# First conv pairs from scaled x while the shift loads, and twenty modulation tiles on TensorE

## The chip, the cores and the metric

The kernel runs on one core of a Trainium2 chip. The metric is device time in microseconds (us). The engines are TensorE (PE; PEld is its weight loads), VectorE (DVE), ScalarE (ACT), GpSimd (POOL) and SyncE (SP), which issues most DMAs.

## The reference, cut to what matters

Two transformer blocks over 256 tokens of width 1024 in float32. Only the head of the first block bears on the change:

```python
mod = silu(c) @ w_ada + b_ada                     # 1024 x 6144
sh1, sc1, g1, sh2, sc2, g2 = split(mod, 6)
h = layer_norm(x) * (1 + sc1) + sh1
z, xbc, dt_raw, sc_b, sc_c, sc_h, gate_a, gate_b = split(h @ w_in)
xbc = silu(causal_depthwise_conv(xbc, ssd_conv_w) + ssd_conv_b)   # 4 taps, 4096 channels
```

Then follow a selective scan over xbc, a short gated convolution, gates, an output projection, a mixture of 64 experts, and a second block (its own `c_2`, `w_ada_2`). Each block needs six modulation rows of 1024, 12 in all. Since the shift is one value per feature for all tokens, (a + sh1) @ W = a @ W + sh1 @ W, and sh1 @ W is one value per output channel.

## The kernel before, in words

**Weights.** `Stream` (L35) loads weights in tiles of 128 x 2048 (1 MB) into a ring of five buffers, `wraw`, through SP in the order in which they were requested; a request waits until a buffer is free (`pump`, L67; `done`, L85). SP's program order is the order of the requests. A linear weight is taken in two halves; each half is split into a high part (`whi`, ScalarE, L196) and a low part (`wlo`, VectorE, L200), both fp32r, three buffers each. `take` (L107) splits one half ahead.

**A pair.** `lin_fm` (L548) makes a pair of 128-channel blocks for 256 tokens: for each half 8 k-tiles times three matmuls (high x high, high weight x low feature, low weight x high feature), so 48 matmuls of 256 columns. The features are `hh` and `hl`, high and low part of h, features on partitions.

**Modulation.** One row of 1024 is a "piece" of four tiles of 1 MB (two k-tiles each). The first two, shift `sh1` = piece (0,0) and scale `sc1` = piece (0,1), are computed by TensorE in `ada_piece` (L395): per k-tile four matmuls with 32 stationary columns in four column groups, 8 per tile, which the trace shows as 16 instructions. The other ten pieces are 40 tiles. They are requested between the weights at places given by strings (L270: x for the 16 conv pairs, s for 12 gated-conv pairs, o for 4, z for 8, g for 8, u for 8) and worked on by `ada_tick` (L410) after the pair of the same place: the first k-tile of a piece on ScalarE (L430), the other seven on VectorE (L432, multiply by silu(c) and add into `adac`, later `adae`), then one sum over partitions with ones on TensorE (L437) and the bias (L392).

**The start.** SP loads c, shift tiles with x behind the second, scale tiles, then the first conv weights. `norm_rows` normalises x, `turn_rows` (L498) transposes it into four PSUM tiles, `to_feature` (L508) scales and shifts them and makes `hh` and `hl`. Every matmul of the conv pairs needs both sc1 and sh1.

**Order.** The order on SP is that of the program. On the other engines a planner takes, by its own costs and due times, the earliest instruction of the program that it holds ready. Once built, each engine runs in order.

**The stages** up to 454 us: start; 16 conv pairs (`xbc_pair`, L621) with four taps on ScalarE and VectorE (L631, L633) and the dt product (L567); 12 gated-conv pairs interleaved with the scan (`ssd`, L654); 4 pairs `pyb`; 8 pairs z; 8 pairs of gates; 4 times two pairs with `w_ssd_out`; `w_o`, whose rows are multiplied by g1 on VectorE (L242).

Of the kernel before, what the change touches and what calls it, by code (L numbers as in the profile page):

```python
# [18 lines left out]
F32 = mybir.dt.float32  # L19
# [7 lines left out]
T = 256  # L27
# [7 lines left out]
class Stream:  # L35
# [31 lines left out]
    def pump(self):  # L67
        while self.issued < len(self.reqs):
            i = self.issued
            load, _, tag = self.reqs[i]  # L70
            tag = tag or (self.free or [None])[0]
            if tag not in self.free:
                break
            self.free.remove(tag)
            self.tag[i] = tag
            pool, depth = self.rings[tag]
            if tag == "whl":
                t = [pool.tile([128, 1024], F32, tag=h, name=f"{h}_{i}", bufs=depth) for h in ("whi", "wlo")]
            else:
                t = pool.tile([128, 2048], F32, tag=tag, name=f"{tag}{i}", bufs=depth)  # L80
            load(t)
            self.raw[i] = t
            self.issued += 1

    def done(self, i):  # L85
        self.left[i] -= 1
        if self.left[i] == 0:
            self.raw.pop(i)
            self.free.append(self.tag[i])
            self.pump()  # L90
# [31 lines left out]
def build(ctx, tc, I, out, dbg=None, stop=None):  # L122
# [44 lines left out]
    V.memset(onescol[:, 7:8], 1.0)  # L167
    V.tensor_scalar(ones_r, jp, 0.0, 1.0, op0=OP.mult, op1=OP.add)
    flip = glob.tile([128, 128], F32, name="flip")
# [34 lines left out]

    def req_cols(w, c0, k0=0):
# [4 lines left out]
        ws.add(f, [lambda t, h=h: t.rearrange("p (k n) -> p k n", k=8)[:, :, 128 * h:128 * h + 128] for h in range(2)])  # L210

# [35 lines left out]
    def req_ada_tile(b, piece, k0):  # L247
        w = I["w_ada_2" if b else "w_ada"][0]

        def f(t):  # L250
            n = 2 if (b, piece, k0) == (0, 1, 6) else 1
            for m in range(n):
                nc.sync.dma_start(t.rearrange("p (k n) -> p k n", k=2)[:, 2 // n * m:2 // n * (m + 1)],
                                  w[k0 * 128:(k0 + 2) * 128, piece * 1024:(piece + 1) * 1024]
                                  .rearrange("(k p) n -> p k n", p=128)[:, 2 // n * m:2 // n * (m + 1)])
            if (b, piece, k0) == (0, 0, 2):
                nc.sync.dma_start(x, I["x"][0].rearrange("(t p) d -> p t d", p=128))

        ada_q[b, piece, k0] = ws.add(f, None)

    def req_ada(b, piece):
        for k0 in range(0, 8, 2):
# [28 lines left out]
    for i, c0 in enumerate(bcols + xcols):  # L291
        req_cols(w_in, c0)
        req_ada_at("x", i)
    for i in range(4):
# [71 lines left out]

    hp3 = keep.tile([128, 3, 32], F32, name="hp3")
    for k, nm in enumerate(("ssd_dt_bias", "ssd_A_log", "ssd_D")):
        a = I[nm][0]
        A.dma_start(hp3[:, k, :], bass.AP(tensor=a.tensor, offset=a.offset, ap=[[0, 128], [1, 32]]))  # L370
    Dcol = keep.tile([128, 16], F32, name="Dcol")
    for j in range(2):
        V.tensor_copy(Dcol[64 * j:64 * j + 64], hp3[64 * j:64 * j + 64, 2, j::2])
    Abc = keep.tile([128, 32], F32, name="Abc")
    A.activation(Abc, hp3[:, 1, :], AF.Exp)
    V.tensor_scalar(Abc, Abc, -1.0, None, op0=OP.mult)


# [11 lines left out]
    def ada_end(b, pc, p):  # L390
        r = work.tile([128, 256], F32, tag="adar", name=f"adar{b}_{pc}", bufs=2)
        V.tensor_add(r, p[:, :256], bada[pc % 2])  # L392
        return r

    def ada_piece(b, pc):  # L395

        ada_bias(b, pc)
        p = paux(f"ada{b}_{pc}")
        for k0 in range(0, 8, 2):
            i = ada_q[b, pc, k0]  # L400
            w = ws.take_raw(i)
            wv = w.rearrange("p (k n) -> p k n", k=2)
            for k in range(2):
                for j in range(4):
                    PE.matmul(p[32 * j:32 * j + 32, :256], cst[:, 8 * b + k0 + k, :], wv[:, k, 256 * j:256 * j + 256],
                              start=(k0 + k == 0), stop=(k0 + k == 7), tile_position=(0, 32 * j))
            ws.done(i)
        return ada_end(b, pc, p)

    def ada_tick(*at):  # L410

        for _ in range(ada_at.get(at, 0)):
# [94 lines left out]

    def to_feature(ps, sc, sh, hi, lo, name):  # L508

        for kp, p in enumerate(ps):  # L510
            f = work.tile([128, 2, 256], F32, tag=("scm", "cu")[kp % 2], name=f"{name}_tf{kp}", bufs=2)
            for k in range(2):
                kk = 2 * kp + k
                scale_shift(k, f[:, k, :], p[:, 256 * k:256 * k + 256], sc[:, kk:kk + 1], sh[:, kk:kk + 1])
            hilo(f, hi[:, 2 * kp:2 * kp + 2, :], lo[:, 2 * kp:2 * kp + 2, :])
# [7 lines left out]
    hh = keep.tile([128, 8, T], F32R, tag="actH", name="hh")  # L523
    hl = keep.tile([128, 8, T], F32R, tag="actL", name="hl")
    ws._split(0)
    to_feature(xnt, sc1, sh1, hh, hl, "h")


# [30 lines left out]


    dt = keep.tile([128, 2, 32], F32, name="dt")
    dA = keep.tile([128, 2, 32], F32, name="dA")
# [4 lines left out]
    def dt_work():  # L567
        wdt = work.tile([128, 8, 32], F32, name="wdt", tag="X", bufs=2)
        with nc.allow_non_contiguous_dma("dt columns"):
# [3 lines left out]
        hilo(wdt, wdh, wdl)  # L573
        pdt = paux("pdt")
# [42 lines left out]

    BC = keep.tile([128, 16, T], F32, tag="big1", name="BC")
    xs = tail.tile([128, 16, T], F32, tag="big2", name="xs")

    def xbc_pair(dst, f0, d0):  # L621

        p = plin()
        lin_fm(p, hh, hl)

        def evac():
            a = work.tile([128, 2, T], F32, tag="cacc", name=f"cacc{f0}", bufs=2)
            for f in range(2):
                fc = f0 + f
                o = f * T  # L630
                A.activation(a[:, f, :], p[:, o:o + T], AF.Identity, bias=cb[:, fc:fc + 1], scale=cw[:, 96 + fc:97 + fc])  # L631
                for s in (1, 2, 3):
                    V.scalar_tensor_tensor(a[:, f, s:], p[:, o:o + T - s],  # L633
                                           cw[:, (3 - s) * 32 + fc:(3 - s) * 32 + fc + 1],
                                           a[:, f, s:], op0=OP.mult, op1=OP.add)
            A.activation(dst[:, d0:d0 + 2, :], a, AF.Silu)

        defer(evac)

    adac = tail.tile([128, 2, D], F32, tag="ga", name="adac")  # L640
    for i in range(16):
        if i < 8:
# [3 lines left out]
        ada_tick("x", i)  # L646
        if i >= 2:
            step()
# [1345 lines left out]
```

## Time and profile before

| | us |
|---|---|
| Median of 3 runs (lowest, highest) | 1335.69 (1335.33, 1337.22) |
| The profiled execution, own time | 1335.36 |
| Its span, first to last instruction | 1333.5 |
| PE / PEld / DVE / ACT / POOL busy | 1265.9 / 1026.6 / 813.2 / 562.3 / 178.3 |
| Mean granted clock of TensorE | 0.981 |

A matmul's end is modelled in this trace: a row of 0.28 us is a matmul that the next one follows after less. The distance of starts is what one costs, and a busy TensorE need not be at its peak. "<-DVE ..." names what ended an engine's idle time.

### The profile page before, as it was taken

Reading aid. Unit: us, or ns where it says so; the run is one execution under the profiler, and the core shown is the slowest. Engines: PE = TensorE matmul, PEld = TensorE weight load, DVE = VectorE, ACT = ScalarE, POOL = GpSimd, SP = SyncE. Lnnn points to the kernel's source line nnn. Section 1 sums busy time; section 2 is a strip of 40 time slices with the busy share of each in tenths; the row PEclk is TensorE's granted clock in tenths of the full one; section 3 lists DMA queues with packets and bytes.
Section 4 is the critical chain, followed back from the end, with each engine's and each line's share of the span. In section 5 each row is a group of like instructions: output and inputs, shape, how many; then the busy total and the mean of one; then the engine's idle time right before and its main releaser. Section 6 shows DMA issues by size and latency. Waiting matters only on the chain.

```text
span 1333.5 us, 22547 instructions
## 1 busy us (share of the span) xinstructions
PE 1265.9 (95%) x8998; PEld 1026.6 (77%) x8998; DVE 813.2 (61%) x1306; ACT 562.3 (42%) x849; POOL 178.3 (13%) x169
## 2 busy tenths in 40 slices
PE   4999999999999989999999999999979998999997
PEld 2989988789899777657576767476548876999985
DVE  2999998977898852222322222222255677788995
ACT  1666644455654341313131313132245655666643
POOL 1001243421100000211112111112120000000000
PEclk9899999999999969999999999999989999999999
DMA  9977867669789287999999999999995334455450
GB/s 338 323 232 254 263 220 239 226 196 320 250 281 362 78 352 296 406 417 419 419 418 413 400 418 419 378 421 403 418 347 179 126 127 141 144 190 190 161 187 32
DMA packets 148975, 380.18 MB, mean 285 GB/s; under 512 B 7839, under 2 KB 97285, under 8 KB 129028
## 3 DMA queue, kind: packets, MB, share of 16 engines
q1 hardware_dynamic: 145856, 373.20, 75.7%
q0 software_dynamic: 2240, 5.34, 1.2%
q8 instruction: 71, 1.16, 0.4%
q10 hardware_dynamic: 772, 0.19, 0.1%
q14 instruction: 36, 0.29, 0.1%
HBM read 377.59 MB, written 1.10 MB: 284 GB/s over the span
## 4 chain that ended last, share of the span: by engine, by line
PE 61%; DVE 5%; DMA 3%; issue 2%; ACT 1%; POOL 0%; POOLq 0%; DVEq 0%; SPq 0%; ACTq 0%
PE gu L1444 16%; PE dn L1475 8%; PE xgp L1402 5%; PE sc L1497 4%; PE pgt L556 2%; PE pgt L557 2%; PE pgt L558 2%; PE pvl L557 2%; PE pvl L556 2%; PE pvl L558 2%; PE pf L908 1%; PE pf L910 1%; PE pf L906 1%; DVE wlo L200 1%; DMA wraw<-in_w_down_dram 1%
## 5 line engine op out<-in xcount | busy, mean ns | idle before, releaser
L196 ACT ACTIVATE whi<-wraw 128x1024 fp32r<-128x1024 f32 x216 | 228.2, 1059 | 239.6 <-PE pf L910 30.8
L200 DVE TENSOR_TENSOR wlo<-wraw,whi 128x1024 fp32r<-128x1024 f32 x216 | 271.4, 1259 | 64.4 <-ACT whi L196 63.0
L1444 PE MATMUL gu<-mraw,xg 128*32 128x256 f32 (+2 forms) x976 | 135.1, 381 | 0.0
L1485 POOL TENSOR_TENSOR y<-yf,y 128x512 fp32r<-128x512 f32 x60 | 76.9, 1282 | 420.8 <-ACT y L1484 420.7
L1454 DVE SCALAR_TENSOR_TENSOR act<-act,gc,gu 128x256 f32<-128x256 f32 x31 | 14.9, 480 | 192.9 <-ACT act L1453 192.9
L1484 ACT ACTIVATE y<-yf 128x512 fp32r<-128x512 f32 x62 | 39.1, 630 | 160.4 <-DVE yf L1483 160.4
L1444 PEld LDWEIGHTS gu<-mraw,xg 128*32 128x32 f32 (+2 forms) x976 | 86.7, 135 | 22.7 <-issue 5.3
L1444 PE MATMUL gu<-wraw,xg 128*32 128x256 f32 (+2 forms) x704 | 98.7, 381 | 0.0
L1483 DVE TENSOR_TENSOR yf<-dn,g 128x512 f32<-128x512 f32 x62 | 42.9, 692 | 66.2 <-PE dn L1475 66.2
L558 PE MATMUL pl<-hh,wlo 128*128 128x256 f32 x256 | 74.3, 291 | 4.2 <-DVE wlo L200 4.1
L1444 PEld LDWEIGHTS gu<-wraw,xg 128*32 128x32 f32 (+2 forms) x704 | 58.2, 129 | 24.1 <-issue 3.9
L556 PE MATMUL pl<-hh,whi 128*128 128x256 f32 x256 | 73.7, 288 | 0.0
L557 PE MATMUL pl<-hl,whi 128*128 128x256 f32 x256 | 73.5, 288 | 0.0
L432 DVE SCALAR_TENSOR_TENSOR adac<-wraw,csil,adac 128x1024 f32<-128x1024 f32 x49 | 66.4, 1355 | 5.1 <-DMA wraw<-in_w_ada_dram 4.5
L1497 PE MATMUL sc<-y,S 128*128 128x512 f32 x248 | 63.3, 404 | 1.4 <-ACT y L1484 0.8
L1497 PEld LDWEIGHTS sc<-y,S 128*128 128x128 f32 x248 | 45.5, 188 | 17.7 <-issue 4.4
L1453 ACT ACTIVATE act<-gu 128x256 f32<-128x256 f32 x31 | 11.9, 384 | 107.3 <-PE gu L1444 107.3
L1404 ACT ACTIVATE xg<-xgp,mvp 128x512 f32<-128x512 f32 (+1 forms) x64 | 48.8, 765 | 19.4 <-PE xgp L1402 19.2
L1402 PE MATMUL xgp<-D,x2h 128*128 128x512 f32 (+1 forms) x128 | 55.5, 434 | 1.4 <-DVE D L1121 1.4
L1475 PE MATMUL dn<-mraw,aT 128*32 128x512 f32 (+2 forms) x200 | 55.4, 596 | 0.0
L558 PEld LDWEIGHTS pl<-hh,wlo 128*128 128x128 f32 x256 | 49.5, 194 | 6.2 <-DVE wlo L200 5.8
L1402 PE MATMUL xgp<-D,x2l 128*128 128x512 f32 (+1 forms) x128 | 53.8, 421 | 0.1
(575 smaller groups left out, 3522.8 us busy)
## 6 DMA issues: line engine op xcount, KB each, us to landing
wraw<-in_w_in_dram SPq DMA_DIRECT2D x56, 1024.0 KB, 6.2
wraw<-in_w_ada_dram SPq DMA_DIRECT2D x47, 1024.0 KB, 7.6
wraw<-in_w_up_dram SPq DMA_DIRECT2D x44, 1024.0 KB, 5.3
wraw<-in_w_down_dram SPq DMA_DIRECT2D x37, 1024.0 KB, 10.0
mraw<-in_w_up_dram SPq DMA_DIRECT2D x32, 1024.0 KB, 14.5
mraw<-in_w_gate_dram SPq DMA_DIRECT2D x28, 1024.0 KB, 7.1
mraw<-in_w_down_dram SPq DMA_DIRECT2D x23, 1024.0 KB, 17.4
wraw<-in_w_gate_dram SPq DMA_DIRECT2D x21, 1024.0 KB, 15.1
```

What stands on the lines that cost most here:

```text
L196: A.activation(hi, v, AF.Copy)
L200: V.tensor_sub(lo, v, hi.bitcast(F32))
L432: V.scalar_tensor_tensor(acc, wv[:, k, s_], c, acc, op0=OP.mult, op1=OP.add)
L556: PE.matmul(o, wh[:, k, :], xh[:, k0 + k, :], start=(k == 0), stop=False)
L557: PE.matmul(o, wh[:, k, :], xl[:, k0 + k, :], start=False, stop=False)
L558: PE.matmul(o, wl[:, k, :], xh[:, k0 + k, :], start=False, stop=(k == 7))
L1402: PE.matmul(p[:, :c1 - c0], src[:, t, j::8], Dt[:, t, c0:c1], start=(q == 0), stop=(q == 3))
L1404: A.activation(xg[:, j, c0:c1], p[:, :c1 - c0], AF.Identity, scale=mvp[:, 1, j:j + 1], bias=mvp[:, 0, j:j + 1])
L1444: PE.matmul(p[c * k:c * k + c, off:off + 256], xg[:, j, 128 * bb + c * k:128 * bb + c * k + c], wt[j], start=(j == 0), stop=(j == 7), tile ...
L1475: last_dn[0] = PE.matmul(pd[h][c * k:c * k + c, :], aT[:, j, c * k:c * k + c], wt[j][:, 512 * h:512 * h + 512], start=(j == 0), stop=(j == ...
L1485: last_sub[0] = (V if b >= LAST else G).tensor_sub(y[:, 1, hs_], yf[:, h, :], y[:, 0, hs_].bitcast(F32))
L1497: PE.matmul(p, St[:, bb + m, 128 * t:128 * t + 128], y[:, k, 512 * h:512 * h + 512], start=(q == 0), stop=(q == 2 * len(ys) - 1))
```

## The change

- The scale tiles are loaded first, with x behind the first of them; then the weights of the first three conv pairs (NF = 3), into rooms of their own (not ring buffers); then the shift tiles; then the stream as before.
- x times scale, without shift, is split into `vv[0]` (high, ScalarE) and `vv[1]` (low, VectorE), and also kept in float32 (`scaled`). The first three pairs take `vv` for their features. TensorE's order for this part is written out: the first pair with k outside and its two halves inside, shift tiles in `ada_rows` between the halves of pairs 2 and 3.
- When the shift is there, TensorE multiplies it with the raw weights of the three pairs (`prow`); `shift_cols` turns the rows into columns, `shift_evac` corrects the first three tokens and adds the rest as a bias in Silu. `hh` and `hl` are made from `scaled` and the shift for all later work.
- The first five of the ten pieces (20 tiles, those of stages x, s and o) go to TensorE in `ada_tick`, in `ada_rows`. The strings change; each stage keeps its number of tiles.
- The three small DMAs of dt bias, A and D, with what hangs on them, come after the features; the dt weights load after the norm. Constants are put ahead of the norm's statistics. `cst` goes: the stationary columns are a broadcast of `csil`.

```diff
@@ Stream.pump
+            if isinstance(tag, tuple):
+                load(tag[0])
+                self.raw[i] = tag[0]
+                self.tag[i] = None
+                self.issued += 1
+                continue
@@ requests
-            n = 2 if (b, piece, k0) == (0, 1, 6) else 1
+            n = 2 if (b, piece, k0) == (0, 0, 6) else 1
-            if (b, piece, k0) == (0, 0, 2):
+            if (b, piece, k0) == (0, 1, 0):
                 nc.sync.dma_start(x, ...)
-    req_ada(0, 0)
-    req_ada(0, 1)
+    req_ada(0, 1)
+    NF = 3
+    w01 = tail.tile([128, 2, 2048], F32, tag="big2", name="w01")
+    wrooms = [w01[:, 0, :], w01[:, 1, :], tail.tile([128, 2048], F32, tag="yb", name="w2")]
+    for i in range(NF):
+        req_cols(w_in, XBC0 + 2048 + 256 * i, 0, (wrooms[i],))
+    req_ada(0, 0)
-   "0110110110110110,010101010101,1111,11111111,11111111,10101010"
+   "0000111101111011,110111100000,1111,11111111,11111111,01010101"
@@ modulation
+    def ada_rows(p, b, pc, k0):
+        i = ada_q[b, pc, k0]
+        wv = ws.take_raw(i).rearrange("p (k n) -> p k n", k=2)
+        for k in range(2):
+            c = csil[:, 8 * b + k0 + k:8 * b + k0 + k + 1].to_broadcast([128, 32])
+            for j in range(4):
+                PE.matmul(p[32 * j:32 * j + 32, :256], c, wv[:, k, 256 * j:256 * j + 256],
+                          start=(k0 + k == 0), stop=(k0 + k == 7), tile_position=(0, 32 * j))
+        ws.done(i)
@@ ada_tick
+            if n < ADA_PE:                      # ADA_PE = 5
+                if k0 == 0:
+                    ada_acc[0] = pacc(f"ada{b}_{pc}")
+                ada_rows(ada_acc[0], b, pc, k0)
+                if k0 == 6:
+                    ada_row(ada_end(b, pc, ada_acc[0]), b, pc)
+                continue
@@ start
     norm_rows(x, xn, 1e-5, "ln0")
-    r0 = ada_piece(0, 0)
-    sh1 = ada_cols(r0, "sh1")
     xnt = turn_rows(xn, "h")
-    r1 = ada_piece(0, 1)
-    sc1 = ada_cols(r1, "sc1", 1.0)
-    ws._split(0)
-    to_feature(xnt, sc1, sh1, hh, hl, "h")
+    sc1 = ada_cols(ada_piece(0, 1), "sc1", 1.0)
+    for kp, p in enumerate(xnt):
+        for k in range(2):
+            kk = 2 * kp + k
+            A.activation(vv[:, 0, kk, :], p[...], AF.Copy, scale=sc1[:, kk:kk + 1])
+            V.scalar_tensor_tensor(vv[:, 1, kk, :], p[...], sc1[:, kk:kk + 1], vv[:, 0, kk, :], op0=OP.mult, op1=OP.subtract)
+        if kp == 1:
+            ws._split(0)
+        for k in range(2):
+            if k:
+                V.tensor_scalar(scaled[kp][:, k, :], p[...], sc1[:, kk:kk + 1], None, op0=OP.mult)
+            else:
+                A.activation(scaled[kp][:, k, :], p[...], AF.Copy, scale=sc1[:, kk:kk + 1])
@@ after lin_fm: three() is its three matmuls on vv, taps() the four conv taps
+    ada_bias(0, 0)
+    pe_order = tc.manual_schedule(engines={mybir.EngineType.SP, mybir.EngineType.PE})
+    pe_order.__enter__()
+    pf = [plin(f"pl{i}") for i in range(NF)]
+    p0b = paux("pl0b")
+    wv_ = [ws.take(), ws.take()]
+    for k in range(8):
+        for f in range(2):
+            three((pf[0] if f == 0 else p0b)[:, :T], wv_[f], k)
+    psh1 = paux("ada0_0")
+    ada_rows(psh1, 0, 0, 0)
+    for i in (1, 2):
+        for f in range(2):
+            w = ws.take()
+            for k in range(8):
+                three(pf[i][:, T * f:T * f + T], w, k)
+                if (i, f, k) == (2, 1, 3):
+                    sh1 = ada_cols(r0, "sh1")
+            if (i, f) != (2, 1):
+                ada_rows(psh1, 0, 0, 2 + 2 * (2 * (i - 1) + f))
+            if (i, f) == (2, 0):
+                r0 = ada_end(0, 0, psh1)
+            if f == 0:
+                for g in range(2):
+                    taps(...)                   # of the pair before
+    for i in range(NF):                         # shift times raw weights, into prow0, prow1
+        for k in range(8):
+            j = k % 4
+            PE.matmul(o[32 * j:32 * j + 32, :], sh1[:, k:k + 1].to_broadcast([128, 32]), w[:, k, :],
+                      start=(k < 4), stop=(k >= 4), tile_position=(0, 32 * j))
+    pe_order.__exit__(None, None, None)
+    ws._split(0)
+    for kk in range(8):
+        f = scaled[kk // 2][:, kk % 2, :]
+        turned = (A.activation(hh[:, kk, :], f, AF.Identity, bias=sh1[:, kk:kk + 1]),
+                  V.scalar_tensor_tensor(hl[:, kk, :], f, sh1[:, kk:kk + 1], hh[:, kk, :], op0=OP.add, op1=OP.subtract))
@@ conv loop
-    for i in range(16):
+    for i in range(NF, 16):
+        if i == NF + 1:
+            shift_cols()
+        elif i in (NF + 2, NF + 3, NF + 4):
+            shift_evac(i - NF - 2)
...
-        if i >= 2:
+        if i >= NF + 1:
             step()
```

`shift_cols` copies `prow` out of PSUM, makes six one-column products with a column `selc` that has a one at every 32nd partition, and forms per-channel constants. `step` advances the dt chain and the scan.

## Rows read from the trace of the kernel before

**Rows 1.** The page's chain that ended last, shares of the span by engine.
```profile
PE 61%; DVE 5%; DMA 3%; issue 2%; ACT 1%; POOL 0%; POOLq 0%; DVEq 0%; SPq 0%; ACTq 0%
```
**Rows 2.** Busy time by stretch: length, PE, PEld, DVE, ACT, POOL, clock, DMA, GB/s.
```profile
15.00:35.50 20.50, 13.82 (x150) 6.63 (x151) 8.19 (x20) 2.98 (x6) 1.91 (x3) 0.95 1.05 392
35.50:57.40 21.90, 21.90 (x167) 21.59 (x166) 19.02 (x26) 13.36 (x18) 0.00 (x0) 0.89 0.94 327
57.40:144.00 86.60, 82.39 (x662) 79.43 (x660) 82.72 (x146) 57.61 (x80) 10.96 (x8) 0.98 0.79 258
144.00:239.00 95.00, 90.00 (x758) 84.64 (x757) 90.31 (x108) 46.94 (x68) 33.92 (x22) 1.00 0.71 231
239.00:282.80 43.80, 39.23 (x322) 34.23 (x321) 39.03 (x41) 17.93 (x29) 17.26 (x15) 1.00 0.66 218
282.80:392.50 109.70, 108.24 (x862) 98.97 (x860) 92.91 (x120) 61.56 (x79) 13.16 (x17) 1.00 0.82 270
```
**Rows 3.** Waits of TensorE, 57.4 to 282.8 us: total us, times, longest.
```profile
PE yp L717 <- DVE Cs L706: 6.2, 4, 2.1
PE pl L558 <- DVE wlo L200: 4.1, 5, 2.9
PE yp L713 <- DVE E L691: 1.4, 1, 1.4
...
```
**Rows 4.** Timeline of the start, 30.5 to 37.5 us: start, length, instruction.
```profile
30.60 0.64 PE L405 MATMUL ada<-wraw,cst 128*32 128x256 f32 x8 [0.98 <-DMA wraw<-in_w_ada_dram]
...
31.87 0.41 PE L452 MATMUL ac_sc<-ident,adar 128*128 128x128 f32 x2 [0.64 <-DVE adar L392]
...
32.52 1.48 ACT L496 ACTIVATE h_tf<-h_tp,sh,sc 128x256 f32<-128x256 f32 x3 [17.89 <-DVE sc L455]
...
34.41 1.06 ACT L196 ACTIVATE whi<-wraw 128x1024 fp32r<-128x1024 f32 x1
...
34.57 0.42 PE L576 MATMUL pdt<-hh,wdh 128*32 128x256 f32 x1 [2.29 <-ACT hh L488]
...
35.49 1.23 DVE L200 TENSOR_TENSOR wlo<-wraw,whi 128x1024 fp32r<-128x1024 f32 x1 [0.25 <-ACT whi L196]
...
35.73 0.41 PE L556 MATMUL pl<-hh,whi 128*128 128x256 f32 x1
```
**Rows 5.** Busy time by stretch, around the first conv matmuls.
```profile
33.40:40.30 6.90, 5.42 (x25) 4.92 (x26) 6.65 (x11) 6.90 (x11) 0.00 (x0) 0.51 1.08 371
```
**Rows 6.** Timeline of TensorE around one closing sum.
```profile
76.92 0.28 PE L556 MATMUL pl<-hh,whi 128*128 128x256 f32 x1
77.13 0.64 PE L437 MATMUL ada<-adac,ones_r 128*32 128x256 f32 x8
77.70 0.38 PE L557 MATMUL pl<-hl,whi 128*128 128x256 f32 x1
77.92 0.28 PE L558 MATMUL pl<-hh,wlo 128*128 128x256 f32 x1
```
**Rows 7.** Timeline of TensorE in one pair after another, first and last row.
```profile
392.97 0.28 PE L556 MATMUL pya<-ynh,whi 128*128 128x256 f32 x1
...
403.52 0.28 PE L557 MATMUL pya<-ynl,whi 128*128 128x256 f32 x1
```
**Rows 8.** Timeline of TensorE: two modulation tiles in a row.
```profile
24.30 1.93 PE L405 MATMUL ada<-wraw,cst 128*32 128x256 f32 x32
```
**Rows 9.** Groups by line, 35.5 to 282.8 us: busy us, mean ns, idle before.
```profile
L432 DVE SCALAR_TENSOR_TENSOR adac<-wraw,csil,adac 128x1024 f32<-128x1024 f32 x40 | 54.8, 1370 | 2.1 <-DMA wraw<-in_w_ada_dram 1.9
...
L196 ACT ACTIVATE whi<-wraw 128x1024 fp32r<-128x1024 f32 x66 | 69.8, 1059 | 78.8 <-PE pl L557 26.2 <-PE pyb L557 22.7 <-PE ph L557 15.6
...
L430 ACT ACTIVATE adac<-wraw,csil 128x1024 f32<-128x1024 f32 x6 | 6.9, 1142 | 3.6 <-DMA wraw<-in_w_ada_dram 3.6
```
**Rows 10.** Timeline of VectorE, 421 to 431 us: the last modulation tile's first half.
```profile
422.11 1.41 DVE L432 SCALAR_TENSOR_TENSOR adae<-wraw,csil,adae 128x512 f32<-128x512 f32 x2 [0.70 <-DMA wraw<-in_w_ada_dram]
```

More of the change, by code (lines that the diff above doesn't have):

```diff
@@ L86, in done @@
         self.left[i] -= 1
-        if self.left[i] == 0:
+        if self.left[i] == 0 and self.tag[i]:
             self.raw.pop(i)
@@ L365, in bcast_row @@
         return t
[L367 to L376, printed above, removed]
     bada = [keep.tile([128, 256], F32, name=f"bada{k}") for k in range(2)]
@@ L399, in ada_piece @@
         for k0 in range(0, 8, 2):
[L400 to L407, printed above, removed]
+            ada_rows(p, b, pc, k0)
         return ada_end(b, pc, p)
@@ L558, in lin_fm @@
                 PE.matmul(o, wl[:, k, :], xh[:, k0 + k, :], start=False, stop=(k == 7))
+    BC = keep.tile([128, 16, T], F32, tag="big1", name="BC")
+    ca = tail.tile([128, NF, 2, T], F32, tag="ga", name="ca")
+    cw4 = cw.rearrange("p (t f) -> p f t", t=4)[:, 16:16 + 2 * NF, :]
+    cws = keep.tile([128, 2 * NF, 4], F32, name="cws")
+    V.tensor_copy(cws[:, :, 0], cw4[:, :, 0])
+    for k in (1, 2, 3):
+        V.tensor_add(cws[:, :, k], cws[:, :, k - 1], cw4[:, :, k])
+    selc = keep.tile([128, 1], F32, name="selc")
@@ new lines, in three @@
+    def three(o, w, k):
+        wh, wl = w
+        PE.matmul(o, wh[:, k, :], vv[:, 0, k, :], start=(k == 0), stop=False)
+        PE.matmul(o, wh[:, k, :], vv[:, 1, k, :], start=False, stop=False)
+        PE.matmul(o, wl[:, k, :], vv[:, 0, k, :], start=False, stop=(k == 7))
+    ada_bias(0, 0)
[4 more added lines that the diff above has]
+    wv_ = [ws.take(), ws.take()]
@@ new lines, in build @@
+    prow1 = [paux("prow0"), paux("prow1")]
+    for i in range(NF):
+        o = prow1[i // 2][:, 256 * (i % 2):256 * (i % 2) + 256]
+        w = wrooms[i].rearrange("p (k n) -> p k n", k=8)
+        for k in range(8):
[3 more added lines that the diff above has]
+    pe_order.__exit__(None, None, None)
+    hh = keep.tile([128, 8, T], F32R, tag="actH", name="hh")
@@ new lines, in build @@
+    hl = keep.tile([128, 8, T], F32R, tag="actL", name="hl")
+    ws._split(0)
+    for kk in range(8):
+        f = scaled[kk // 2][:, kk % 2, :]
+        turned = (A.activation(hh[:, kk, :], f, AF.Identity, bias=sh1[:, kk:kk + 1]),
+                  V.scalar_tensor_tensor(hl[:, kk, :], f, sh1[:, kk:kk + 1], hh[:, kk, :].bitcast(F32),
+                                         op0=OP.add, op1=OP.subtract))
+    hp3 = keep.tile([128, 3, 32], F32, name="hp3")
+    for k, nm in enumerate(("ssd_dt_bias", "ssd_A_log", "ssd_D")):
+        a = I[nm][0]
+        with tc.issue_after(turned[0].ins):
+            A.dma_start(hp3[:, k, :], bass.AP(tensor=a.tensor, offset=a.offset, ap=[[0, 128], [1, 32]]))
@@ new lines, in build @@
+    Dcol = keep.tile([128, 16], F32, name="Dcol")
+    for j in range(2):
+        with tc.issue_after(turned[1].ins):
+            V.tensor_copy(Dcol[64 * j:64 * j + 64], hp3[64 * j:64 * j + 64, 2, j::2])
+    Abc = keep.tile([128, 32], F32, name="Abc")
+    A.activation(Abc, hp3[:, 1, :], AF.Exp)
+    V.tensor_scalar(Abc, Abc, -1.0, None, op0=OP.mult)
+    with tc.issue_after(turned[0].ins), tc.issue_after(turned[1].ins):
+        for g in range(2):
+            taps(ca[:, 2], pf[2], 20 + g, g)
@@ new lines, in build, with shift_cols @@
+    rws = [work.tile([128, 512], F32, tag="E", name=f"rws{i}", bufs=3) for i in range(2)]
+    pcb = paux("pcb")
+    cbias = keep.tile([128, 2, 2 * NF], F32, name="cbias")
+    cedge = keep.tile([128, 2 * NF, 3], F32, name="cedge")
+    def shift_cols():
+        for i in range(2):
+            n = 256 * (NF - 2 * i) if i else 512
+            V.tensor_copy(rws[i][:, :n], prow1[i][:, :n])
+            for m in range(n // 128):
+                PE.matmul(pcb[:, 4 * i + m:4 * i + m + 1], rws[i][:, 128 * m:128 * m + 128], selc, start=True, stop=True)
+        V.tensor_copy(cbias[:, 0, :], pcb[:, :2 * NF])
+        V.tensor_mul(cbias[:, 1, :], cbias[:, 0, :], cws[:, :, 3])
+        for t in range(3):
+            V.tensor_mul(cedge[:, :, t], cbias[:, 0, :], cws[:, :, 2 - t])
@@ L628, in evac @@
             for f in range(2):
[L629 to L635, printed above, removed]
+                taps(a, p, f0 + f, f)
             A.activation(dst[:, d0:d0 + 2, :], a, AF.Silu)
```

59 lines of the change are left out of this document (37 added, 22 removed).

## The prediction

> **What bounds the kernel now.** I read the chain's shares first [rows 1]: TensorE is on the chain far more than anything else. Then busy time by stretch [rows 2], because the change lies in the first 454 us only and shares of the whole span hide it. Four things stand there. Up to 35.5 us the DMA rows are full (share 1.05, 392 GB/s), and TensorE works in pieces. From 35.5 us on TensorE is busy nearly always. From 57.4 to 282.8 us it is idle for 4.2 + 5.0 + 4.6 = 13.8 us (length minus busy time of three rows). In the same three rows VectorE is busy 82.7 of 86.6, 90.3 of 95.0 and 39.0 of 43.8 us. So two engines are nearly full there, and the question is which one sets the pace. The waits of TensorE [rows 3] name VectorE, but their sum is 11.7 us of 225. In the other direction ScalarE waits 78.8 us in front of its weight splits, most of it for matmuls to give the split buffers back [rows 9]: the splits run ahead of TensorE. TensorE therefore sets the pace between the waits of rows 3, and work added to it has to be paid for; work taken from VectorE is worth at most the waits.
>
> **The start.** Today the last modulation tile is used at 30.60 us and ScalarE begins on the features at 32.52 [rows 4]. After the change four tiles fewer are loaded ahead of that point: 4.19 MB at 392 GB/s [rows 2] is 10.7 us, so the last scale tile is used at 19.9. It is whole and no longer halved, 0.4 us more (8 instructions more, worked out below), and 1.9 us follow as today: the features begin at 22.2.
>
> What has to happen before the conv matmuls flow: ScalarE's Copies, in program order, are vv 0 and 1, one scaled, vv 2 and 3, the first weight split, then one scaled, two vv, one scaled, two vv, one scaled, and only then the split of the second half. Twelve at 0.49 us (1.48 for three) and two splits at 1.06 [rows 4] are 8.0 us, and the VectorE half of the second split adds 1.2, less overlap: some 8.8 us after the features begin, that is 31.0 us. The order on TensorE is written out, and in it the second half stands right behind the first three matmuls (k outside, f inside), so the first half, ready at about 26, can't run ahead. Today the flow begins at 35.73 [rows 4]. The gain is 4.7 us, not the 10.7 of the loads. Bounds: 9 us if the planner puts the second split ahead of the later Copies, 3 if the scale comes a little later.
>
> Against it stands work on TensorE that today lies in its idle time ahead of 35 us, or isn't there. A row of 32 instructions of the modulation kind takes 1.93 us [rows 8], one of 8 takes 0.64 [rows 6]: 24 instructions are 1.29 us, so 8 stream in 0.43. In the middle of conv matmuls 8 of them push the next but one matmul from 0.24 to 1.00 us (76.92 to 77.92, rows 6): 0.76. A tile has 16, so 0.76 + 0.43 = 1.19 us. The four shift tiles are 4.8 us. The raw-weight rows are three times 16 of the same kind, with one pair of edges: 3 x 0.86 + 0.3 = 2.9. The two transposes for the shift's columns are 0.4; the six one-column products later some 1.0 (an estimate, between 0.5 and 2).
>
> Steady pace of the conv matmuls: 88 steps from 392.97 to 403.52 are 0.12 us each [rows 7]. Today 167 recorded instructions, three pairs (144) and the dt product, are done at 57.4 [rows 2]. After: 31.0, and 138 matmuls left x 0.12 = 16.6, the low clock again 2.0 (granted 0.51 up to 40.3, rows 5, so the first 4.5 us of the flow ran at 1.2 GHz), 4.8, 2.9 and 0.4 give 57.7, and the dt product, which now needs the shift, is still to come: 24 x 0.12 = 2.9, and the 1.0. That is 61.6 against 57.4: **+4.2 us**, bounds -3 and +7. The features with shift cost eight ScalarE and eight VectorE operations more (4 us each side by side), behind the last conv half and the raw rows; I take them as hidden, and 2 us are late if not.
>
> One rule bears on the clock. The 0.51 was granted after TensorE had stood idle from 32.3 to 34.6 [rows 4, 5]. The Trainium skill, "TensorE: Matmul & The Clock Gate", section "Part 1: The HAM clock gate", says that low is the default and that activity lifts it; the trace agrees (idle, then 0.51). By it the first pair pays the 2.0 us again, as counted; if the scale tiles kept the clock up it would be 2.0 less.
>
> **Twenty tiles on TensorE.** Removed from VectorE: today a piece of four tiles takes one ScalarE operation (1.14 us) and seven on VectorE (1.37), [rows 9]; five pieces are 35 x 1.37 = 48 us of VectorE and 5.7 of ScalarE. Removed from TensorE: five closing sums of 0.76, 3.8 us. Added to TensorE: 20 tiles of 0.86 (streaming alone) to 1.19 (both edges). Some stand beside the scan's matmuls, which have such edges already; I take 1.1: 22.0 - 3.8 = **+18.2 us**, bounds +13.5 and +22.
>
> The row shows 0.76 us for 8 instructions where 0.43 streams, so 0.33 at the two edges. The Trainium skill, "TensorEngine Tiling (Array Packing)", section "Key Properties", says that a change of tiling mode drains the engine; the trace agrees, with those 0.33 us. By the rule at every tile the term is 20.0, without it 13.5.
>
> What the freed VectorE gives back: the 13.8 us of idle time, and 1.7 us of low clock (0.98 over 86.6 us, rows 2) that follows the longest wait: 15.5. The stretch from 282.8 to 392.5, with less on VectorE, still has 1.5 us of idle time, so not all goes; I take **-14 us**. Bounds: -6 (the waits for Cs and E come from a chain ScalarE-VectorE-TensorE, not from load alone), -20 (ends of matmuls are modelled, so some waits may not show). What is late next: with VectorE at 70-75% nothing but TensorE. New waits: a tile on TensorE that hasn't landed stops the conv matmuls queued behind it, where today VectorE waited (2.1 us in all, rows 9); a piece's first tile waits for the sum of the piece before to leave its only bank, a pair of matmuls earlier. Nothing for both, up to 4 in the range.
>
> **The other edits.** Four modulation requests move behind the second of two weight loads near 400-425 us. VectorE's four accumulations of the last tile, 0.7 us each [rows 10], then fall where it is busy without a gap, as gating and splitting of the next weights start: 0 to 2.9 us, I take **+0.6**. Three small DMAs of ScalarE's queue and the 128 KB dt load leave the start and come later: VectorE's first constants no longer wait for one of them, and nothing on the path needs them; 0, gain bounded by 1.5 us on the scale tiles. The stretches from 282.8 on keep their work, and their start moves with the end of this one.
>
> **Sum.** 4.2 + 18.2 - 14.0 + 0.6 = +9.0 us. The profiled execution took 1335.36 us (span 1333.5 and 1.9 around it), 0.3 below the median of the runs. 1344.4; I say 1344.5.
>
> **Rivals.** *VectorE is what sets the pace.* For it: its three rows are as full as TensorE's, and every wait in rows 3 but small ones names it. Then the second split comes early (start -1), the tiles cost what they stream (+13.5), and all waits, hidden ones too, go (-19): -6.5, about 1329. Against it: the 78.8 us that ScalarE waits for TensorE. It decides if TensorE's added work stays under some 22 us beside 20 regained; chance 0.24. *It cancels.* Start +2, tiles at 1.0 (+16.2), waits -18: +0.2, about 1335.7; chance 0.16. *The waits stay.* If the scan's waits are latency and tiles are late on TensorE, -6 takes the place of -14 and 4 us come on top: +21 at worst, with tiles at 1.0 and a start of +3 about +15, 1350; chance 0.13. *The change doesn't do what it says*, in that the planner holds the first pair until the shift is there: the flow would begin no earlier than today, +4.7 more, 1349; in the range of the one before. My forecast, +3 to +13 us, has the remaining 0.47.
>
> **Range and chances.** This kernel's runs can tell about 0.2% (2.7 us) from no change. Slower by more: 0.47 + 0.13 = 0.60; within: 0.16; faster: 0.24. The range reaches the first rival at its upper end and the third nearly whole: 1329 to 1354; the forecast's own is 1338 to 1349.
>
> **What would show it.** Start right: first conv matmul of the flow near 31 us with a gap of several us behind the first three, fourth pair near 58; wrong if the flow begins below 28. Tiles right: some 1.1 us between the conv matmuls on either side of a tile; wrong if below 0.9. Waits right: VectorE near 75% busy from 60 to 280 us, idle time of TensorE below 3 us there, and the z stage beginning some 8 us later than today. If it begins earlier, the sum is wrong on its sign.

## The result, and the profile after

The changed kernel took 1347.03 us (median of 13 runs, 1341.12 to 1354.52) beside 1339.36 us of the kernel before on the same chip (13 runs, 1334.15 to 1343.39): ratio 1.0064, 95% interval 1.0042 to 1.0085. It is slower by 0.64%, or 8.6 us (the medians alone differ by 7.7); the forecast was +9.0 us on 1335.36. The profiled execution took 1350.54 us (span 1348.7), 15.2 more than the one before: 7.7, and it lies 3.5 above its own median while the one before lies 4.0 below its own. A difference between two single profiles is therefore not yet a cost, and what follows takes each part from several kernels.

The chain of waits of the kernel after, shares of the span by engine, against [rows 1]:
```profile
PE 85%; DVE 6%; DMA 4%; issue 2%; ACT 1%; POOL 1%; SPq 0%; DVEq 0%; POOLq 0%; ACTq 0%
```
The two rows can't be held against each other. The chain of the kernel before can be followed back only to 356.49 us (974 of 1333.5 us, its shares add up to 72%), that of the kernel after to 0.74 us; from 420 us on TensorE has 85% of either. So [rows 1] says nothing of the stretch that the change touches, and what sets the pace there has to be read from busy time and waits. Busy time by stretch of the kernel after, columns as in [rows 2]:
```profile
15.00:35.50 20.50, 13.79 (x89) 11.43 (x88) 9.50 (x18) 7.43 (x15) 0.64 (x2) 0.75 1.06 376
35.50:57.40 21.90, 21.90 (x233) 17.63 (x232) 15.00 (x27) 11.78 (x20) 0.55 (x1) 1.00 0.83 262
57.40:144.00 86.60, 86.60 (x792) 79.88 (x791) 71.67 (x148) 57.03 (x82) 7.15 (x6) 1.00 0.79 260
144.00:239.00 95.00, 93.96 (x834) 84.54 (x834) 67.07 (x85) 42.87 (x63) 26.85 (x23) 1.00 0.66 211
239.00:282.80 43.80, 41.63 (x360) 35.07 (x359) 31.82 (x37) 18.50 (x30) 19.03 (x16) 1.00 0.59 200
```
From 57.4 to 282.8 us TensorE's idle time fell from 13.8 to 3.2 us (0 + 1.0 + 2.2), the clock of the first of these stretches rose from 0.98 to 1.00, and VectorE is busy 170.6 of 225.4 us, 76%. What TensorE still waits for there (total us, times, longest), where [rows 3] had 11.7 us, and the two groups by line that answer to [rows 9]:
```profile
PE yp L838 <- DVE Cs L827: 1.6, 2, 1.0
PE pyb L571 <- DVE vv L502: 1.2, 1, 1.2
PE yp L834 <- DVE E L812: 0.3, 1, 0.3
```
```profile
L200 ACT ACTIVATE whi<-wraw 128x1024 fp32r<-128x1024 f32 x59 | 62.4, 1057 | 77.2 <-PE pl L571 18.3 <-PE ph L571 17.4 <-PE pc L571 12.2
...
L445 DVE SCALAR_TENSOR_TENSOR adac<-wraw,csil,adac 128x1024 f32<-128x1024 f32 x1 | 1.7, 1671 | 0.9 <-ACT adac L443 0.9
```
Nearly all of the 40 wide accumulations are gone from VectorE, and ScalarE still waits 77.2 us in front of its weight splits, as it did 78.8 us before. TensorE, not VectorE, paces this stretch.

The start of the kernel after, timeline of TensorE, and then of ScalarE, against [rows 4]:
```profile
26.32 0.55 PE L596 MATMUL pl<-vv,whi 128*128 128x256 f32 x1 [4.55 <-DVE h_tf L538]
...
27.36 0.41 PE L597 MATMUL pl0b<-vv,whi 128*128 128x256 f32 x1
29.39 0.58 PE L598 MATMUL pl0b<-vv,wlo 128*128 128x256 f32 x1 [1.61 <-DVE wlo L204]
29.77 0.42 PE L596 MATMUL pl<-vv,whi 128*128 128x256 f32 x1
...
30.41 0.41 PE L596 MATMUL pl0b<-vv,whi 128*128 128x256 f32 x1
...
53.89 2.80 PE L632 MATMUL prow<-w,sh 128*32 128x256 f32 x48
56.62 0.39 PE L570 MATMUL pl<-hh,whi 128*128 128x256 f32 x1
...
62.30 0.28 PE L572 MATMUL pl<-hh,wlo 128*128 128x256 f32 x1
62.42 1.39 PE L670 MATMUL pcb<-selc,rws 128*128 128x1 f32 x12
63.67 0.36 PE L570 MATMUL pl<-hh,whi 128*128 128x256 f32 x1
```
```profile
22.01 1.57 ACT L530 ACTIVATE vv<-h_tp,sc 128x256 fp32r<-128x256 f32 x4 [17.73 <-DVE sc L468]
23.45 1.07 ACT L200 ACTIVATE whi<-w 128x1024 fp32r<-128x1024 f32 x1
24.40 0.49 ACT L540 ACTIVATE h_tf<-h_tp,sc 128x256 f32<-128x256 f32 x1
24.76 1.23 ACT L530 ACTIVATE vv<-h_tp,sc 128x256 fp32r<-128x256 f32 x3
25.83 1.10 ACT L200 ACTIVATE whi<-w 128x1024 fp32r<-128x1024 f32 x1
```
The features begin at 22.01 (counted: 22.2). The second weight split (the second L200) comes at 25.83, ahead of the last Copies, where the prediction had put it behind all of them; TensorE stops for its lower half for 1.61 us after five matmuls and flows from 29.39. The clock of the flow's first part, same columns as the stretches:
```profile
25.40:35.60 10.20, 7.66 (x34) 7.40 (x35) 5.86 (x11) 4.04 (x8) 0.00 (x0) 0.50 1.04 404
```
One modulation tile between the conv matmuls, timeline of TensorE, against [rows 6]:
```profile
78.83 0.28 PE L572 MATMUL pl<-hh,wlo 128*128 128x256 f32 x1
79.04 1.07 PE L403 MATMUL ada<-wraw,csil 128*32 128x256 f32 x16
80.04 0.39 PE L570 MATMUL pl<-hh,whi 128*128 128x256 f32 x1
80.27 0.28 PE L571 MATMUL pl<-hl,whi 128*128 128x256 f32 x1
```
From 78.83 to the next but one matmul it is 1.44 us where 0.24 is the steady pace: a tile costs 1.2 us, the upper of the two bounds.

### The profile page after: what moved, and what is told of

Read it like the earlier page. It is cut to its first block, busy times and chain, and to the rows that moved or that the text cites. A ratio compares the mean times of both kernels' runs of the same rounds, so it can differ in the third digit from the quotient of the medians.

```text
span 1348.7 us, 23251 instructions
## 1 busy us (share of the span) xinstructions
PE 1291.1 (96%) x9338; PEld 1038.5 (77%) x9338; DVE 781.2 (58%) x1298; ACT 562.4 (42%) x859; POOL 169.8 (13%) x169
## 4 chain that ended last, share of the span: by engine, by line
PE 85%; DVE 6%; DMA 4%; issue 2%; ACT 1%; POOL 1%; SPq 0%; DVEq 0%; POOLq 0%; ACTq 0%
PE gu L1565 16%; PE dn L1596 8%; PE xgp L1523 5%; PE sc L1618 4%; PE pl L570 2%; PE ada L403 2%; PE pl L571 2%; PE pl L572 2%; PE pgt L570 2%; PE pgt L571 2%; PE pgt L572 2%; PE pvl L570 2%; PE pvl L572 2%; PE pvl L571 2%; PE pf L1029 1%
## 5 line engine op out<-in xcount | busy, mean ns | idle before, releaser
L200 ACT ACTIVATE whi<-wraw 128x1024 fp32r<-128x1024 f32 x210 | 221.9, 1058 | 251.4 <-PE pf L1031 30.8
L204 DVE TENSOR_TENSOR wlo<-wraw,whi 128x1024 fp32r<-128x1024 f32 x210 | 259.2, 1235 | 99.9 <-ACT whi L200 93.3
L570 PE MATMUL pl<-hh,whi 128*128 128x256 f32 x208 | 59.4, 285 | 0.0
L571 PE MATMUL pl<-hl,whi 128*128 128x256 f32 x208 | 58.3, 280 | 0.0
L572 PE MATMUL pl<-hh,wlo 128*128 128x256 f32 x208 | 58.2, 280 | 0.0
L1596 PE MATMUL dn<-wraw,aT 128*32 128x512 f32 (+2 forms) x208 | 51.9, 596 | 1.3 <-DMA wraw<-in_w_down_dram 1.3
L570 PE MATMUL pgt<-h3h,whi 128*128 128x256 f32 x176 | 50.7, 288 | 0.6 <-ACT h3h L502 0.6
```

Of the source, the lines that this page charges most:

```text
L200: A.activation(hi, v, AF.Copy)
L204: V.tensor_sub(lo, v, hi.bitcast(F32))
L570: PE.matmul(o, wh[:, k, :], xh[:, k0 + k, :], start=(k == 0), stop=False)
L571: PE.matmul(o, wh[:, k, :], xl[:, k0 + k, :], start=False, stop=False)
L572: PE.matmul(o, wl[:, k, :], xh[:, k0 + k, :], start=False, stop=(k == 7))
L1596: last_dn[0] = PE.matmul(pd[h][c * k:c * k + c, :], aT[:, j, c * k:c * k + c], wt[j][:, 512 * h:512 * h + 512], start=(j == 0), stop=(j == ...
```

## Experiments

All of these compute the whole reference. "Measured" gives the ratio to the kernel before on the same chip, with its 95% interval; times at a place come from the one profile of each kernel. Three marks are used: the start of the flow of conv matmuls, of the fourth conv pair, and of the z stage. With the new start the dt product (24 x 0.12 = 2.9) and the one-column products (62.30 to 63.67 less one step, 1.25), 4.1 us, lie behind the fourth pair; with the old they lie ahead of it or don't exist.

**The twenty tiles alone.**
```diff
 # kernel before
+ADA_PE = 5
+if n < ADA_PE: ada_rows(ada_acc[0], b, pc, k0) ...   # five pieces of four tiles on TensorE
```


> The kernel before with nothing changed but the twenty tiles of stages x, s and o on TensorE (strings and start as before). Theory (TensorE sets the pace there): 20 tiles cost some 1.2 us each and five closing sums of 0.76 go, +20; TensorE's idle time from 57 to 283 us falls from 13.8 to about 2 us; the z stage begins 4 to 8 us later than the 282.9 us of before, and the whole is 0.3 to 0.6% slower. Rival (VectorE sets the pace): the z stage begins 3 to 7 us earlier and the whole is faster by 0.2 to 0.5%.


Measured: 1.0057 [1.0039, 1.0075]. The z stage began at 288.0 where it was 282.9. TensorE's idle time over 57.4 to 282.8 us is 3.15 and VectorE's busy time 169.7, as in the kernel after; busy time over the one stretch:
```profile
57.40:282.80 225.40, 222.25 (x1966) 201.03 (x1965) 169.68 (x253) 114.72 (x166) 54.09 (x44) 1.00 0.68 226
```
Tiles alone bring most of the loss. "VectorE sets the pace" would have made this kernel faster; it falls.

**The start with four tiles.**
```diff
 # kernel after
-ADA_PE = 5
+ADA_PE = 1
```


> The changed kernel with only the first piece (4 tiles) on TensorE, the other 16 tiles back on VectorE. Theory: the fourth conv pair begins where it does in the changed kernel (56.6 us) and the start alone costs 3 to 4 us; the z stage begins near 287 to 291 us, since what TensorE saves (16 x 1.2 less 3.0, 16 us) comes back as waits for VectorE of 10 to 16 us; whole 0.2 to 0.6% slower than before. Rival (VectorE sets the pace): VectorE has 16 x 2.6 = 41 us more, and the z stage begins 10 us or more later than the 290 of the changed kernel; over 1% slower than before.


Measured: 1.0041 [1.0024, 1.0059]; z stage at 286.5, 3.8 us ahead of the kernel after. With sixteen tiles back on VectorE its busy time and TensorE's idle time return (12.5 us):
```profile
57.40:282.80 225.40, 212.90 (x1784) 198.58 (x1783) 204.54 (x298) 124.58 (x178) 58.23 (x43) 0.98 0.72 238
```

**The first pair's halves one after the other.**
```diff
 # kernel after, first pair
-for k in range(8):
-    for f in range(2):
+for f in range(2):
+    for k in range(8):
```


> The changed kernel, first conv pair with its first half's 24 matmuls ahead of the second half's. Theory: the flow begins near 26.3 us and not 29.4, since only the second half waits for its split; the fourth pair begins 2 to 3 us earlier than 56.6, near 54, and the whole is 2 to 3 us below the changed kernel. Rival (the scaled features arrive too late for a half on its own, or the low clock lasts as long as before): fourth pair at 56 or later, no gain.


Measured: 1.0035 [1.0017, 1.0053]. The flow begins at 25.9 instead of 29.4. The fourth pair begins at 53.3; over all profiles it is 52.9 to 54.0 us in three with this order and 54.7 to 56.6 in four with the other, so the loop order costs about 2 us.

**The u requests.** In the kernel after moved back, and in the kernel before moved alone:
```diff
 # us_back: kernel after          # u_only: kernel before, the other way round
-"...,11111111,01010101"
+"...,11111111,10101010"
```


> The changed kernel with the modulation requests of the last eight places (u) as before, behind the first of two weight loads. Theory: the way from the first w_ssd_out matmul to the last of w_o is 0 to 3 us shorter than in the changed kernel; nothing before it moves. Rival: that stretch is the same or longer, and the 2 us that the changed kernel takes more there come from elsewhere.

> The kernel before with nothing changed but the places of the modulation requests among the w_ssd_out loads, as in the changed kernel. Theory: from the first w_ssd_out matmul to the last of w_o it takes 73.5 us and not 71.5 (four profiles with the new places show 73.2 to 73.6 but for none, six with the old ones 71.0 to 71.9), nothing ahead of it moves, whole +0.1 to +0.2%. Rival: that stretch is longer only where stages x to o were changed too; here 71.5.


Measured: 1.0053 [1.0033, 1.0072] for the first, beside 1.0064 with the requests moved; 1.0017 [0.9997, 1.0038] for the second. Neither ratio by itself tells it from nothing. The stretch from the first matmul of w_ssd_out to the last of w_o does: 73.6 (kernel after), 73.2 (halves one after the other), 73.6 (four tiles) and 73.4 us (requests alone) with the new places, 71.0 to 72.0 in the nine profiles with the old. One more kernel with the new places, further below, has 71.8. The cause in the kernel after, timeline of VectorE and of TensorE:
```profile
420.11 0.68 DVE L502 TENSOR_TENSOR ml<-mg,mh 128x512 fp32r<-128x512 f32 x1
427.12 0.75 DVE L445 SCALAR_TENSOR_TENSOR adae<-wraw,csil,adae 128x512 f32<-128x512 f32 x1 [6.32 <-DMA wraw<-in_w_ada_dram]
427.79 1.22 DVE L204 TENSOR_TENSOR wlo<-wraw,whi 128x1024 fp32r<-128x1024 f32 x1
```
```profile
429.06 0.39 PE L572 MATMUL pya<-ynh,wlo 128*128 128x256 f32 x1 [2.39 <-DVE wlo L204]
```
VectorE stands 6.32 us in front of a modulation tile that hasn't landed. Queued behind it is the split of a weight (427.79), and TensorE waits 2.39 us for that split, where the kernel before lost 0.5 us at this place. The requests alone show the same two rows (6.26 and 2.16 us). What makes up the rest of the 2 us differs: in the requests alone and in the four tiles a low clock follows that wait, in the other two TensorE waits once more, at the start of w_o. Busy time of the requests alone, and timeline of TensorE in the kernel after:
```profile
426.10:429.50 3.40, 3.40 (x19) 3.40 (x18) 3.37 (x6) 0.41 (x1) 0.00 (x0) 0.50 0.62 187
```
```profile
456.01 0.51 PE L1027 MATMUL pmix<-whi,mh 128*128 128x512 f32 x1 [0.78 <-DVE adar L393]
```

**Eight tiles, in two places, and twelve.** Pieces are numbered 0 to 4 in the order of use: 0 and 1 lie in the conv stage, 2 between 120 and 157 us, 3 and 4 behind that, in the scan's stage.
```diff
 # kernel before with the code of twenty tiles
-if n < ADA_PE:
+if n in (0, 1):        # tiles8_x;  (3, 4): tiles8_so;  (2, 3, 4): tiles12_so
```


> The kernel before with the first two pieces (8 tiles, all in the x stage) on TensorE. Theory (a tile costs TensorE 1.2 us and gives back only the waits that stand in its own stage): 8 x 1.2 less two closing sums is 8.0 us; the x stage has 4.1 us of waits and 1.7 of low clock to give back; the gated-conv pairs begin 2 us later than the 143.8 of before and the z stage 2 to 3 us later than 282.9; whole +0.1 to +0.3%. Rival (the first tiles taken from VectorE are worth most, whatever their stage): z stage 2 to 5 us earlier.

> The kernel before with the fourth and fifth piece (the last 4 tiles of the s stage and the 4 of the o stage) on TensorE. Theory: again 8.0 us, against 4.9 us of waits in the s stage and 4.4 in the o stage, of which 2 to 3 stay (the scan's own chain): z stage between 1 us earlier and 3 us later than 282.9. If the hidden waits are as large as the visible ones: 3 to 5 us earlier, and this is faster than before. Rival (what a tile gives back is the same anywhere): the same as with the 8 tiles in the x stage.

> The kernel before with the third to fifth piece on TensorE (2 tiles at the end of x, 6 of s, 4 of o). Theory: 12 x 1.2 less three sums is 12.1 us against at most 9.3 of visible waits: z stage 3 to 6 us later than 282.9, whole +0.2 to +0.4%. Rival (VectorE sets the pace in s and o): z stage earlier than with 8 tiles.


Measured: 0.9979 [0.9964, 0.9994], 0.9978 [0.9960, 0.9997] and 1.0051 [1.0030, 1.0072]. Eight tiles in either place are faster than the kernel before by about 0.2%; that was not expected. Twelve, with piece 2 among them, lose nearly as much as twenty. Busy time by stretch with eight tiles in the conv stage, to be held against [rows 2]:
```profile
57.40:144.00 86.60, 86.60 (x768) 81.48 (x767) 74.49 (x139) 55.34 (x77) 7.16 (x6) 1.00 0.84 273
144.00:239.00 95.00, 90.30 (x761) 85.05 (x760) 87.61 (x104) 49.11 (x69) 33.70 (x24) 1.00 0.68 222
239.00:282.80 43.80, 39.23 (x323) 34.31 (x322) 39.03 (x41) 17.91 (x28) 16.89 (x14) 1.00 0.66 215
```
All 4.2 us of idle time of the conv stage went, and with it the 3.4 us at 0.50; the scan's remained. What such a stretch costs can be read from the start of the kernel after: at 0.50 the conv matmuls follow each other after 0.213 us (29.77 to 30.41, three steps), where 0.12 is the steady pace, so 44% of it is lost, 1.5 us of 3.4. The table has the time up to the z stage with this taken off, from the first matmul of the flow (old start) or from the fourth pair less the 4.1 us (new start). For the kernel before: 282.85 - 35.73 = 247.1, with 8.0 us at 0.50 (35.7 to 40.3, and 3.4 from 101.7 on), less 3.5, is 243.6.

| tiles on TensorE | old start, from the flow | new start, from the fourth pair |
|---|---|---|
| 0 | 243.6 (before), 243.6 (requests alone) | |
| 4 | | 224.0 |
| 8 | 244.9 (conv), 244.4 (scan), 244.1 (conv, later normalization) | 223.1 |
| 12 | 249.4 (pieces 2, 3, 4) | 227.6 (pieces 0, 3, 4) |
| 20 | 250.2 | 229.5 (kernel after) |

Eight tiles add 8 x 1.2 - 2 x 0.76 = 8.1 us to TensorE and make this part about 1 us longer; the idle time that the rows show gave back 4.5 of these in the first of them, and where the rest came from isn't shown. Nor is it shown how a part that is 1 us longer belongs to a kernel that is 0.2%, some 2.8 us, faster. The low clock that goes with the waits is not in the table: it cost 1.5 us in the kernel before, 4.5 in the requests alone, whose code up to there is the same, and 0, 1.5 and 3.0 in the three kernels with eight tiles. How often it comes over many executions isn't known. Piece 2 finds no wait to fill: with pieces 3 and 4 TensorE is idle 4.2 us up to 144 and 1.3 us from there to 239, and with piece 2 as well 4.4 and 1.3, so its tiles are paid in full: 4 x 1.2 - 0.76 = 4.0 us of the 5.0 between 244.4 and 249.4. The ratio rises by more, 0.0073 or 9.8 us; 3.0 us of that profile are a low clock in the gates stage (below), and the rest isn't shown. Sixteen tiles, eight in each place, were not tried.

**The new start in its best form.**
```diff
 # kernel after, halves one after the other, u requests moved back
-if n < ADA_PE:
+if n in (0, 3, 4):     # start_so;  start8: ADA_PE = 2
```


> The changed kernel with the first pair's halves one after the other, the u requests as before, and TensorE tiles only for pieces 1, 4 and 5 (12 tiles; 8 of the twenty are back on VectorE). Theory: fourth pair near 53.3 us as with the halves apart; eight tiles fewer on TensorE save it 8.0 us and bring back up to 5.8 of waits in the x stage: z stage near 284 to 286 us (286.9 with the halves apart and twenty tiles), whole between 0.1 and 0.4% slower than before. Rival (VectorE sets the pace in x): z stage at 288 or later.

> The changed kernel with the first pair's halves apart, the u requests as before, and only the first two pieces (8 tiles) on TensorE. Theory: against twelve tiles (-0.07%, z stage at 287.2) four tiles fewer save TensorE 4 us and give back some of the scan's waits: z stage at 284 to 287, whole -0.2 to +0.1%. Rival: the start is worth nothing, and it is as the 8 tiles without it, -0.2%.


Measured: 0.9993 [0.9978, 1.0008] and 1.0005 [0.9986, 1.0023]. The first was expected slower by 0.1 to 0.4% with the z stage at 284 to 286; it isn't slower, though the z stage began at 287.2. With eight tiles the fourth pair begins at 52.9, where four profiles of the old start without tiles ahead of it have 57.4 to 58.9: of 4.5 to 6.0 us, 4.1 go to the products behind the mark. The z stage begins at 281.7, against 283.2 with eight tiles in the conv stage and the old start (285.1 in another execution of the same code up to there, 3.0 of it low clock). The time isn't better than without the new start (0.9979), and where its 1.5 us go isn't settled: from the last matmul of w_o to the end, which no edit touches, single profiles lie between 866.1 and 875.1 us.

**The normalization of the gates stage one pair later.** In the kernel after, the gates stage (first gate matmul to first of w_ssd_out) took 57.9 us where it was 53.7, with TensorE waiting, and then this, by stretch:
```profile
345.30:403.10 57.80, 55.47 (x419) 51.40 (x418) 49.52 (x72) 32.06 (x41) 3.87 (x6) 0.94 0.79 257
...
366.70:373.50 6.80, 6.80 (x30) 6.36 (x31) 3.99 (x7) 3.04 (x5) 0.00 (x0) 0.50 0.52 157
```
The waits of TensorE in that stage of the kernel after, and below them those of the kernel with the edit:
```profile
PE prs L929 <- ACT rsh L502: 1.4, 1, 1.4
PE pg L572 <- DVE wlo L204: 0.9, 1, 0.9
```
```profile
PE prs L929 <- ACT rsh L502: 0.7, 1, 0.7
PE pg L572 <- DVE wlo L204: 0.4, 1, 0.4
PE prs L930 <- DVE rsl L502: 0.2, 1, 0.2
```
The theory was that the wait for the group scale pulls the clock down. The edit calls the normalization's matmuls a pair later:
```diff
 # gates stage: kernel after (norm_late); kernel before with pieces 0, 1 (tiles8_norm_late)
-else:
-    gnorm(i - 1)
+elif i >= 2:
+    gnorm(i - 2)
 ...
+gnorm(6)
 gnorm(7)
```


> The changed kernel with the normalisation of the scan's groups one pair of gate matmuls later. Theory: TensorE's wait of 2.3 us for the group scale goes, the granted clock stays at its upper level through the gates, and the stretch from the first gate matmul to the first w_ssd_out matmul is 53 to 55 us and not 57.8; whole 2 to 4 us below the changed kernel, 0.3 to 0.5% above before. Rival (the low clock there has another cause): a low stretch near 366 us stays, 57 us.

> The kernel before with the first two pieces on TensorE (8 tiles, x stage) and the normalisation one pair later. Theory: the wait of 1.0 to 1.6 us in the gates goes and low clock there can't follow: 1 to 3 us below the kernel before, beyond the 8 tiles' own -0.2%: -0.2 to -0.4%. Rival: the later normalisation makes the first w_ssd_out matmuls wait for the last groups, 1 to 3 us; then the same as before.


Measured: 1.0029 [1.0011, 1.0047] beside 1.0064 [1.0042, 1.0085] without it (another series); and 0.9981 [0.9960, 1.0003] beside 0.9979, where 1 to 3 us of gain were expected and none is seen. The gates stage, and w_ssd_out with w_o behind it, in the kernel with the edit:
```profile
343.40:397.00 53.60, 52.24 (x420) 48.49 (x419) 48.91 (x71) 31.78 (x41) 3.87 (x6) 1.00 0.87 283
397.00:468.80 71.80, 70.06 (x488) 64.27 (x488) 62.46 (x83) 30.86 (x37) 3.44 (x6) 1.00 0.64 226
```
No low clock, 53.6 us, and the second row (71.8) has lost its 2 us too: VectorE stood 4.2 us for the unlanded tile there and not 6.32, and TensorE waited 0.9 us and not 2.39. That agrees with the theory, but it isn't shown. Of the fourteen profiles six have the 6.8 us of 0.50 in this stage (56.7 to 57.9 us) and eight have not (53.3 to 54.7). In all six the drop begins 0.6 to 1.7 us after the wait for the group scale has ended. By TensorE's idle time there (with the drop 1.45, 1.65, 1.86, 1.92, 2.09 and 2.32 us; without it 0.96 to 1.84) they overlap; and the u requests alone, whose code up to this stage is that of the kernel before, show it where the kernel before doesn't. More idle time goes with the drop more often; which execution has it, no row tells.

## Why the prediction was right

- **What sets the pace**: as read from [rows 2], [rows 3] and [rows 9]; [rows 1], which the prediction names first, doesn't reach back to this stretch and is no ground for it. The idle time fell to 3.2 us (below 3 was said), VectorE to 76% (75%), the z stage came 7.4 us later (8). What the reading left out is that the first tiles are nearly free, and only those behind them cost.
- **Start, +4.2**: 56.62 + 2.88 + 1.25 = 60.75 against 57.43, +3.3 in the two profiles compared; over four profiles each, 54.7 to 56.6 plus 4.1 against 57.4 to 58.9, +1.7 between the means (55.5 and 57.9). The flow began at 29.4, not 31.0, above the 28 that would have refuted it: the planner put the second split early, which the prediction named as a bound. The gap stood behind five matmuls and not three; the raw-weight rows took 2.8 us (2.9). The low clock took back part: 6.2 us of the flow lie ahead of 35.6 at 0.50, worth 2.7 us by the 44%, where 2.0 were counted. And of the first three pairs' 144 matmuls, 141 are left behind the first three, not 138: 0.4 us that the sum lacked.
- **Twenty tiles, +18.2, less 14.0**: +4.2, and without the clock's 1.7 us +5.9. The table has +6.6 (250.2 less 243.6, old start) and +5.5 (229.5 less 224.0, which has four). A tile costs 1.2 us between conv matmuls, where 1.1 was taken for all: 20 x 1.19 - 3.8 = 20.0 in place of 18.2. Given back were 10.6 us of idle time and 1.5 of low clock, 12.1 in place of 14.0. By these rows it would be +7.9 with the clock and +9.4 without, where the table has +6.6; so some 2.8 us more were given back than any row shows, which the prediction had allowed for ("some waits may not show"). The Trainium skill, "TensorEngine Tiling (Array Packing)", section "Key Properties", has a change of tiling mode drain the engine: the trace agrees for every tile between conv matmuls, with 1.2 against 0.86 streaming.
- **u requests, +0.6: mis-sized too.** Measured +2.0, in bounds of 0 to 2.9. The prediction priced four accumulations that stand where VectorE is busy. What costs is the wait of the first of them for its transfer, with a ready split behind it. The prediction had asked that question of TensorE's queue and not of VectorE's.
- **Not foreseen**: the low clock of the gates stage, 3.0 us where it occurs (44% of 6.8; the kernel after needs 57.9 us there and with the requests moved back, where the drop is missing, 54.3; 0.5 of the 3.6 us between them is idle time). The prediction let the stretches from 282.8 on only move.
- **Sum**: the profiles' 15.2 are 7.4 (start of the z stage), -1.0 (z stage itself), 4.2 (gates), 2.1 (w_ssd_out and w_o) and 2.5 (rest). The ratio's 8.6 us shows that not all of this comes in every execution. By the means, 1.7 (start), 6.6 (tiles, old start) and 2.0 (requests) are 10.3, less the low clock of the old stretch (1.5 or 4.5), plus that of the gates stage where it comes (up to 3.0): 5.8 to 11.8. The sum came right to half a microsecond with its start 2.5 too large, its requests 1.4 too small and the gates left out. That it came so close is luck; the sign and the size rest on the tiles.
- **Rivals**: "VectorE sets the pace" and "it cancels" fall with the twenty tiles alone (1.0057, interval from 1.0039 on); at eight tiles (0.9979) the first would have had the sign right. "The waits stay" falls with the idle time. The planner did not hold the first pair: it flowed before the shift was there.

## What to carry to other kernels

Where two engines are both nearly full, moving work from one to the other fills the waits between them first and is paid in full afterwards. Here eight tiles of twenty came out 0.2% faster in either of two places, with waits still left in the other; twelve with piece 2 among them lost 0.5%. So count the waits stage by stage, move work only into a stage that has them, and measure each step: the rows did not show all that was given back. An operation that waits for a transfer costs what is queued behind it on its engine; ask this of every queue, also where the operation itself is short. A gain at the start is kept only as far as what was moved behind it is smaller: here 4.1 of 4.5 to 6.0 us went to products that the old start had already done or didn't need.

## What the hardware showed that was not expected

- Work added to a nearly full engine can cost nothing: TensorE took 8.1 us more, with 13.8 us of idle time in the rows, and the kernel became 0.2% faster in two places (both intervals below 1). Why is not shown.
- The granted clock fell to 0.50 for 6.8 us after waits of only 0.9 and 1.4 us, some 4 us apart, in a stage in which TensorE is busy 96% of the time; and between the fourth pair and the z stage it fell for 3.4 us at a time, three times in one execution (101.9, 183.8 and 228.2 us, requests alone; each within 2 us of a wait of 1.7 to 2.9 us) and once in another of the same code up to there (the kernel before). With twenty tiles between the waits, no profile of five shows it between the fourth pair and the z stage.
- The same code's marks differ between executions: the fourth pair began between 57.4 and 58.9 us in four profiles, and the z stage at 282.9 and at 286.3 in two; 3.0 of these 3.4 us are low clock. A difference of that size between two profiles decides nothing without a row that names it.
